# Two-block kernel: recurrent mixer's products reordered, block 2's set-up inside the second FFN, modulation products pinned

## Chip, cores and metric

One NeuronCore of a Trainium2 chip runs the whole kernel. The metric is the device time of one execution in microseconds; the median of three executions counts.

## What is computed

A token stream x of 256 tokens by 1024 features goes through two blocks, all in float32.

```python
# first block, two layers
x = x + mixer_a(rms_norm(x, norm_mix[0]))       # gated MLP with a 128x128 causal mix
x = x + conv_ffn(rms_norm(x, norm_ffn[0]))      # 1024 -> 2 x 3072 -> 1024
x = x + mixer_b(rms_norm(x, norm_mix[1]))       # recurrent mixer
x = x + conv_ffn(rms_norm(x, norm_ffn[1]))
h = rms_norm(x, norm_final)

# mixer_b, width 1536 in 6 heads of 256
g, xb = split(h @ w_in); g = gelu(g); xb = causal_conv(xb)      # 4 taps
r, i = sigmoid(xb @ w_a + b_a), sigmoid(xb @ w_x + b_x)         # by head
a = exp(8 * r * log_sigmoid(lam))
hs = scan(a, sqrt(1 - a**2) * i * xb)                           # along the tokens
return (hs * g) @ w_out

# second block
sh1, sc1, gt1, sh2, sc2, gt2 = split(silu(c) @ ada_w + ada_b)   # "modulation", v = 0 to 5
xn = rms_norm(h, mix_norm_g) * (1 + sc1) + sh1
h = h + gt1 * second_mixer(xn)              # sparse attention and an RWKV7 time mix
xn2 = rms_norm(h, moe_norm_g) * (1 + sc2) + sh2
return h + gt2 * moe(xn2)                   # router, 2 of 32 experts
```

## The kernel before

**Order of the work.** `first_block` (L695) runs `mixer_a`, `ffn` of layer 0, `mixer_b`, `setup2` and `ffn` of layer 1, then `final_norms`. `build` calls `router_setup` after it, then `second_mixer`, `finish_blocks` and `moe`. Each engine has a queue in order. Nobody writes that queue out by hand: a planner issues what it expects to be ready, and takes the earlier in program order where several are. So an instruction can run long before its place in the program, where its operands, its memory and its bank allow it. The change uses a call, `keep_in_program_order`, that places an instruction not before the one that its engine was given just before it in the program; later ones may still overtake both.

**Products.** Weights come by DMA on SyncE's queue in pieces of 512 KB (`wload`, L244). ScalarE copies each into a rounded high half and VectorE subtracts for the low half (`split_act`, L303 to L306); four split places of two pieces' halves make a ring. `mm3` (L267) makes one float32 product of three passes, L272 to L274. Feature products (`feats`, L286) have 256 token columns; output projections (`out_proj`, L391) have 512.

**Norms.** `ending` (L422) adds the residual by feature halves and calls `after(half)`, which for the mixers and FFNs transposes that half of x (`turned`, L371, L377) and splits it for the next stage. The row factors follow from sums of squares on ScalarE (L334) and Newton steps on VectorE (`newton`, L309). `factor_rows` (L347) puts them in a row: for each token half a diagonal on VectorE (L353) and a product with ones on TensorE (L354); both diagonals use one tile. `final_norms` (L1387) does this for two norms in a row and applies the modulation (L1407 to L1409).

**`mixer_b`** (L564) works in thirds P of four feature blocks: `conv_in` (two times 48 passes), `gelu_in` (the same), `gates` (48 passes), `recur` (ScalarE exponentials and roots, VectorE scans; L621 to L643) and the output projection (48 passes). `recur` of the last third goes by two halves. The order of the program is:

```python
for P in range(4):
    conv_in(P); mod_steps() if P == 0; gelu_in(P); y = recur(P - 1)
    gates(P); side(P); out_proj of y, with ending at P == 3
```

**Modulation.** `mod_load(v, h)` (L780) loads 512 columns of the modulation weights into four of eight tiles. With `summed` VectorE adds up the eight weighted rows at once (L795, L797), else TensorE does it in `mod_steps` (L810). `mod_steps` (L800) turns all halves loaded before it into columns: L822 for v = 0 and 1, L828 for v = 3 and 4, or into a row for v = 2 and 5 (L817, with a bias row loaded and the result written out on SyncE's queue, L816 and L819). It runs at the first step of each FFN, after `conv_in(0)` of `mixer_b`, and in `final_norms`. Loads stand at the end of steps: (0, 0), (0, 1), (2, 0), (2, 1) in FFN 0, (4, 0) and (4, 1) unsummed in `mixer_b`, (3, 0), (3, 1), (5, 0), (5, 1) in FFN 1.

**`setup2`** (L842) zeroes two images in DRAM from a zero tile (L847, L849), loads parameter rows on GpSimd's queue and transposes them (`turn`, L191 to L196), derives columns (L861 to L863), calls `setup_rwkv` (L872: masks, and four transposes for the head table at L909, each with a bank of its own and a copy at L910) and loads two gains. `router_setup` (L1510) loads the router's weights and makes a row and its broadcast with small products (L1523, L1526).

Of the kernel before, what the change touches and what calls it, by code (L numbers as in the profile page):

```python
# [7 lines left out]
F32 = mybir.dt.float32  # L8
# [3 lines left out]
ALU = mybir.AluOpType  # L12
# [5 lines left out]
NT = 2  # L18
# [88 lines left out]
class Net:  # L107
# [415 lines left out]
    def ffn(self, hT, ss, layer, side, after):  # L523
# [6 lines left out]
        with self.scope() as p:  # L530
            acc, hd, rows = None, {}, None
            for s in range(13):
                if s < 12:
# [30 lines left out]
    def mixer_b(self, hT, ss, side, after):  # L564
# [8 lines left out]
        with self.scope() as p:  # L573
# [72 lines left out]

            acc = todo = out_ss = None
            for P in range(4):
                if P < 3:
                    xb, xs = conv_in(P)  # L650
                if P == 0:
                    self.mod_steps()
                if P < 3:
                    gg = gelu_in(P)
                y = recur(P - 1, *todo, 4 if P < 3 else 2) if P > 0 else None
                if P < 3:
                    todo = (xb, gg, *gates(P, xs))
                side(P)
                if P > 0:
                    acc = acc or self.banks()  # L660
                    it = self.items(y, w_out, 4 * (P - 1), 4)
                    self.out_proj(acc, it[:2], P == 1)
                    done = None
                    if P == 3:
                        done, out_ss = self.ending(acc, after)
                    self.out_proj(acc, it[2:], False, done)
            return out_ss
# [27 lines left out]
    def first_block(self):  # L695
# [5 lines left out]
        with self.scope() as self.mod_scope:  # L701
# [39 lines left out]
            def then(i):  # L741
# [5 lines left out]
            ss = self.mixer_b(hT, ss, loads({0: (4, 0), 1: (4, 1)}), then(2))  # L747
            self.setup2()
            final, banks = Scope(self), []
            ss = self.ffn(hT, ss, 1, loads({1: (3, 0, 1), 3: (3, 1, 1), 5: (5, 0, 1), 8: (5, 1, 1)}),  # L750
                          lambda half: self.final_half(final, half, banks))
            self.final_norms(final, ss, banks)
# [27 lines left out]
    def mod_load(self, v, h, summed=False):  # L780
# [17 lines left out]
        self.mod_ready.append((v, h, rows, part))  # L798

    def mod_steps(self, psum=None):  # L800


        nc, psum = self.nc, psum or self.bank
        for v, h, rows, part in self.mod_ready:
            by = self.ones[:, :1]
            if part is None:
                ps, by = psum(), self.sel4
                for k in range(8):
                    q = 32 * (k % 4)
                    nc.tensor.matmul(ps[q:q + 32], self.c_b[:, k], rows[k], start=k < 4, stop=k >= 4, skip_group_check=True)  # L810
                part = self.mod_scope.tile([128, 512], name="mpart")
                nc.scalar.copy(part, ps)
            ps, c0 = psum(), v * D + 512 * h
            if v in (2, 5):
                row = self.mod_scope.tile([1, 512], name="mrow")
                nc.sync.dma_start(row, self.A["ada_b_2"][:, c0:c0 + 512])  # L816
                nc.tensor.matmul(ps[:1], by, part, start=True, stop=True)  # L817
                nc.vector.tensor_tensor(row, row, ps[:1], ALU.add)  # L818
                nc.sync.dma_start(self.mod[v // 3:v // 3 + 1, 512 * h:512 * h + 512], row)  # L819
            elif v < 2:  # L820
                for k in range(4):
                    nc.tensor.matmul(ps[:, k:k + 1], part[:, 128 * k:128 * k + 128], by, start=True, stop=True)  # L822
                to = self.mod_col[:, v, 4 * h:4 * h + 4]
                nc.vector.tensor_tensor(to, to, ps[:, :4], ALU.add)
            else:

                for k in range(8):
                    nc.tensor.matmul(ps[64 * h:64 * h + 64, k:k + 1], part[:, k::8], by, start=True, stop=True)  # L828
# [13 lines left out]
    def setup2(self):  # L842
        nc, A, c = self.nc, self.A, self.const
        self.x_img = [self.dram.tile([32, self.UNIT], F32, name=f"x_img{i}") for i in range(2)]
        with self.scope() as p:
# [9 lines left out]
            v(A[f"rwkv_{n}_2"]) for n in ("w0", "a0", "k_k", "k_a")] + [  # L855
            A["rwkv_r_k_2"][0].rearrange("(n h) p -> n (h p)", h=2), v(A["rwkv_ln_w_2"]), v(A["rwkv_ln_b_2"])], nc.gpsimd)
        self.rc = turn()

# [4 lines left out]
        nc.vector.tensor_scalar(rd[:, 23:27], rc[:, 27:31], -1.0, 1.0, op0=ALU.mult, op1=ALU.add)  # L863
        self.setup_rwkv()

        self.qkg = c.tile([128, 2], F32, name="qkg")
        for i, n in enumerate(("q_norm_g_2", "k_norm_g_2")):
            for h in range(2):
                nc.gpsimd.dma_start(self.qkg[HS[h], i:i + 1], A[n].rearrange("o d -> d o"))
        nc.vector.tensor_scalar(self.qkg[:, 0:1], self.qkg[:, 0:1], 0.125, None, op0=ALU.mult)  # L870

    def setup_rwkv(self):  # L872
# [31 lines left out]
        for b in range(4):  # L904
            nc.vector.tensor_copy(self.hsel[:, b, 2 * b:2 * b + 2], hi[:, :2])
        self.hexp = self.par2.tile([8, 4, 128], F32, name="hexp")
# [480 lines left out]
    def final_norms(self, p, ss, banks):  # L1387
# [13 lines left out]
        self.mod_steps()  # L1401
        gcol, shcol = self.mod_cols(0, 1, self.mix_g)
# [30 lines left out]
    def second_mixer(self):  # L1433
# [10 lines left out]
        with ExitStack() as es:  # L1444
# [14 lines left out]
            with self.scope(first) as zz, self.scope(second) as px:  # L1459
# [51 lines left out]
    def router_setup(self):  # L1511
# [10 lines left out]
        for k in range(8):  # L1522
            nc.tensor.matmul(ps[:1, :36], self.sh2[:, k:k + 1], rw[:, k], start=k == 0, stop=k == 7)  # L1523
        nc.vector.tensor_tensor(row[:1], row[:1], ps[:1, :36], ALU.add)
        ps = self.bank()
        nc.tensor.matmul(ps[:, :36], self.ones[:1], row[:1], start=True, stop=True)  # L1526
        self.r_add = c.tile([128, 36], F32, name="r_add")
# [259 lines left out]
```

## Time and profile before

| what | us |
|---|---|
| median of 3 executions | 1501.7 (1501.48 to 1502.59) |
| the profiled execution | 1502.12 |
| its span, first to last instruction | 1500.4 |
| recurrent mixer, about | 371 to 503 |
| second FFN, about | 508 to 727 |
| second mixer, about | 741 to 1030 |
| experts | to the end |

The profiled execution is 0.42 us over the median, and 1.7 us of it lie around the span. The page gives each engine's busy time and the chain that ended last; the views by stretch, the timelines and the waits are taken from the same execution. PE is TensorE's products, PEld its weight loads, DVE VectorE, ACT ScalarE, POOL GpSimd, SP SyncE. Overlapping starts are normal: products are pipelined and their ends are modelled.

### The profile page before, as it was taken

What the parts mean: (1) busy time and instruction counts of PE and PEld (TensorE: products, weight loads), DVE (VectorE), ACT (ScalarE), POOL (GpSimd) and SP (SyncE); (2) the same over time, 40 slices, a digit from 0 to 9 for tenths busy, and PEclk for the clock granted to TensorE, in tenths of its full rate; (3) what the DMA queues carried; (4) which work ended last, traced back from release to release, by engine and by line L of the source; (5) the groups of instructions that cost most, each with busy time, mean ns of one, the idle gap of its engine ahead of it and who ended that gap; (6) DMA issues with size and microseconds to landing.
All of it is one profiled execution on the core that took longest, in us unless ns stands there. A gap on an engine that the chain in (4) does not pass through costs nothing.

```text
span 1500.4 us, 22885 instructions
## 1 busy us (share of the span) xinstructions
PE 1371.2 (91%) x9085; PEld 1042.1 (69%) x9085; DVE 852.7 (57%) x1628; ACT 615.2 (41%) x955; POOL 32.2 (2%) x63
## 2 busy tenths in 40 slices
PE   7999999999999899999999899998978878879785
PEld 6778999999998689999798688887413313234131
DVE  5796798778788789878859742775201101101011
ACT  6644555556688555555575544552100000000000
POOL 3000000000001000000000100001000000000000
PEclk9999999999999999999899795999999989999998
DMA  9898586555555578563243352487999999999997
GB/s 318 282 327 277 158 274 215 187 187 160 170 182 184 172 272 275 187 191 109 72 153 113 99 121 86 170 336 308 390 421 420 420 420 421 421 421 419 421 419 253
DMA packets 165573, 391.18 MB, mean 261 GB/s; under 512 B 19440, under 2 KB 101100, under 8 KB 141780
## 3 DMA queue, kind: packets, MB, share of 16 engines
q1 hardware_dynamic: 153124, 383.64, 70.2%
q10 hardware_dynamic: 11136, 4.53, 1.3%
q0 software_dynamic: 1200, 1.49, 0.4%
q8 instruction: 73, 1.20, 0.3%
q14 instruction: 40, 0.33, 0.1%
HBM read 386.19 MB, written 3.43 MB: 260 GB/s over the span
## 4 chain that ended last, share of the span: by engine, by line
PE 58%; DMA 29%; DVE 7%; ACT 4%; issue 2%; SPq 0%; POOL 0%; DVEq 0%; ACTq 0%
DMA arena<-expert_w_gate 12%; PE ps L272 9%; PE ps L273 9%; PE ps L274 9%; DMA arena_w<-expert_w_gate 7%; DMA arena_w<-expert_w_down 6%; PE pc L273 5%; PE pc L272 5%; PE pc L274 5%; DMA arena<-expert_w_down 3%; PE pg L272 2%; PE pg L274 2%; PE pg L273 2%; DVE arena_r L306 2%; ACT arena_r L305 1%
## 5 line engine op out<-in xcount | busy, mean ns | idle before, releaser
L305 ACT ACTIVATE arena_r<-arena 128x1024 fp32r<-128x1024 f32 (+2 forms) x330 | 328.9, 1008 | 287.1 <-PE ps L273 73.1
L306 DVE TENSOR_TENSOR arena_r<-arena,arena_r 128x1024 fp32r<-128x1024 f32 (+2 forms) x330 | 376.9, 1154 | 119.2 <-ACT arena_r L305 115.8
L272 PE MATMUL ps<-arena_r,arena_r 128*128 128x256 f32 (+2 forms) x1192 | 353.7, 297 | 1.0 <-DVE arena L818 1.0
L273 PE MATMUL ps<-arena_r,arena_r 128*128 128x256 f32 (+2 forms) x1192 | 352.9, 296 | 1.1 <-DVE arena_r L306 1.1
L274 PE MATMUL ps<-arena_r,arena_r 128*128 128x256 f32 (+2 forms) x1192 | 352.4, 296 | 0.6 <-DVE arena_r L306 0.6
L272 PEld LDWEIGHTS ps<-arena_r,arena_r 128*128 128x128 f32 (+1 forms) x1192 | 229.3, 192 | 10.4 <-issue 3.5
L273 PEld LDWEIGHTS ps<-arena_r,arena_r 128*128 128x128 f32 (+1 forms) x1192 | 229.2, 192 | 7.2 <-DVE arena_r L306 1.5
L274 PEld LDWEIGHTS ps<-arena_r,arena_r 128*128 128x128 f32 (+1 forms) x1192 | 229.2, 192 | 5.6 <-DVE arena_r L306 0.8
L1709 PE MATMUL pc<-arena 128*32 128x512 f32 x576 | 144.4, 672 | 34.1 <-DMA arena<-expert_w_up 18.9
L272 PE MATMUL pc<-arena_r,arena_r 128*128 128x512 f32 x344 | 136.0, 399 | 5.3 <-ACT arena_r L305 3.4
L273 PE MATMUL pc<-arena_r,arena_r 128*128 128x512 f32 x344 | 135.9, 395 | 0.4 <-DVE arena_r L306 0.4
L274 PE MATMUL pc<-arena_r,arena_r 128*128 128x512 f32 x344 | 134.2, 393 | 0.0
L1709 PE MATMUL pc<-arena_w,arena 128*32 128x512 f32 x448 | 117.4, 663 | 15.8 <-DMA arena_w<-expert_w_gate 9.8
L1716 DVE TENSOR_TENSOR arena<-arena,pc 128x512 f32<-128x512 f32 x8 | 5.5, 688 | 204.6 <-PE pc L1709 204.6
L1692 ACT ACTIVATE arena<-ps,mod_col,moe_g 128x128 f32<-128x128 f32 x32 | 14.7, 458 | 246.1 <-DVE arena L1694 246.1
L1709 PEld LDWEIGHTS pc<-arena 128*32 128x32 f32 x576 | 31.4, 120 | 99.1 <-issue 37.1
L272 PE MATMUL pg<-arena_r,arena_r 128*128 128x256 f32 (+1 forms) x312 | 95.0, 306 | 2.0 <-DVE arena L916 1.8
L273 PE MATMUL pg<-arena_r,arena_r 128*128 128x256 f32 (+1 forms) x312 | 94.7, 305 | 1.1 <-DVE arena_r L306 1.1
L274 PE MATMUL pg<-arena_r,arena_r 128*128 128x256 f32 (+1 forms) x312 | 95.1, 306 | 0.2 <-DVE arena_r L306 0.2
L521 DVE SCALAR_TENSOR_TENSOR arena<-arena 128x255 f32<-128x255 f32 (+2 forms) x228 | 94.4, 477 | 0.2
L1735 PE MATMUL pc<-arena 128*32 128x512 f32 (+2 forms) x320 | 74.7, 584 | 11.5 <-DMA arena<-expert_w_down 7.6
L272 PEld LDWEIGHTS pc<-arena_r,arena_r 128*128 128x128 f32 x344 | 65.2, 190 | 19.8 <-ACT arena_r L305 5.1
(451 smaller groups left out, 1688.2 us busy)
## 6 DMA issues: line engine op xcount, KB each, us to landing
arena<-f_w_up SPq DMA_DIRECT2D x96, 512.0 KB, 3.9
arena<-expert_w_gate SPq DMA_DIRECT2D x41, 1024.0 KB, 19.9
arena<-expert_w_down SPq DMA_DIRECT2D x34, 1024.0 KB, 19.9
arena_w<-expert_w_up SPq DMA_DIRECT2D x33, 1024.0 KB, 19.9
arena<-expert_w_up SPq DMA_DIRECT2D x31, 1024.0 KB, 19.9
arena_w<-expert_w_down SPq DMA_DIRECT2D x26, 1024.0 KB, 19.9
arena<-ada_w SPq DMA_DIRECT2D x48, 512.0 KB, 5.6
arena<-f_w_down SPq DMA_DIRECT2D x48, 512.0 KB, 4.2
```

The costliest lines, as they stand in the source:

```text
L272: nc.tensor.matmul(acc, ah, bh, start=first, stop=False, **kw)
L273: nc.tensor.matmul(acc, ah, bl, start=False, stop=False, **kw)
L274: nc.tensor.matmul(acc, al, bh, start=False, stop=last, **kw)
L305: self.nc.scalar.activation(hi, src, AF.Copy)
L306: self.nc.vector.tensor_tensor(lo, src, hi.bitcast(F32), ALU.subtract)
L521: nc.vector.scalar_tensor_tensor(o[:, i:], src[:, :S - i], w[k - 1 - i], o[:, i:], op0=ALU.mult, op1=ALU.add)
L1692: nc.scalar.activation(xg[:, k], ps[:, j], AF.Identity, scale=g, bias=sh)
L1709: nc.tensor.matmul(gu[i][es], xg[:, kk, es], ws[e][:, k], start=kk == 0, stop=kk == 7, skip_group_check=True)
L1716: tt(hd, hd, gu[1], ALU.mult)
L1735: nc.tensor.matmul(o[es], hT[:, k0 + k, es], ws[e][:, k, f0 - c0:f0 - c0 + n], start=k0 + k == 0, stop=k0 + k == 3, skip_group_check=True)
```

## The change

`mixer_b` gets a written order in which the gates come next to the recurrence and the output projection a third later. `mod_steps` runs at the third step of each FFN, at the ninth of the second one, after the first gates of `mixer_b`, and in `second_mixer` after the value projection, in place of `final_norms`; all its products are pinned. `router_setup` goes there too, with pinned products. `setup2` runs in two parts at the fifth and eleventh step of the second FFN. `factor_rows` has two diagonal tiles. The head table is made in one bank with one copy. The Newton steps of `final_norms` work on both token halves in one tile of two columns.

```diff
@@ factor_rows
-            by = p.tile([128, 128], name="fdiag")
+            by = p.tile([128, 128], name="fdiag", bufs=2)
@@ ffn
-                if s == 0:
+                if s == 2 or (s == 8 and layer == 1):
                     self.mod_steps()
@@ mixer_b
-            for P in range(4):
...
+            acc = []
+
+            def out(P, y, done=None):
+                acc.extend(() if acc else self.banks())
+                it = self.items(y, w_out, 4 * P, 4)
+                self.out_proj(acc, it[:2], P == 0)
+                self.out_proj(acc, it[2:], False, done)
+
+            xb, xs = conv_in(0)
+            gg = gelu_in(0)
+            todo = (xb, gg, *gates(0, xs))
+            side(0)
+            self.mod_steps()
+            xb, xs = conv_in(1)
+            side(1)
+            gg = gelu_in(1)
+            y = recur(0, *todo, 4)
+            todo = (xb, gg, *gates(1, xs))
+
+            xb, xs = conv_in(2)
+            out(0, y)
+            y = recur(1, *todo, 4)
+            rg = gates(2, xs)
+            todo = (xb, gelu_in(2), *rg)
+            out(1, y)
+            done, out_ss = self.ending(acc, after)
+            out(2, recur(2, *todo, 2), done)
             return out_ss
@@ first_block
-            self.setup2()
...
+            def beside(s):
+                late(s)
+                if s == 4:
+                    turn.append(self.setup2())
+                if s == 10:
+                    self.setup2_columns(*turn)
+
+            ss = self.ffn(hT, ss, 1, beside, lambda half: self.final_half(final, half, banks))
@@ mod_steps, router_setup
+    def pinned(self, *args, **kw):
+
+        self.tc.keep_in_program_order(self.nc.tensor.matmul(*args, **kw))
...
-                    nc.tensor.matmul(ps[q:q + 32], self.c_b[:, k], rows[k], start=k < 4, stop=k >= 4, skip_group_check=True)
+                    self.pinned(ps[q:q + 32], self.c_b[:, k], rows[k], start=k < 4, stop=k >= 4, skip_group_check=True)
...
         self.mod_ready = []
+        if "mpart" in self.mod_scope.tags:
+            self.mod_scope.drop("mpart")
@@ setup2, which now returns turn; setup2_columns is what stood after turn()
-        self.rc = turn()
...
+    def setup2_columns(self, turn):
+        nc = self.nc
         self.rc = turn()
...
-        for b in range(4):
-            ps = self.psum()
-            nc.tensor.transpose(ps[:8, :128], self.hsel[:, b], self.ident)
-            nc.vector.tensor_copy(self.hexp[:, b], ps[:8, :128])
+        ps = self.psum()
+        for b in range(4):
+            nc.tensor.transpose(ps[:8, 128 * b:128 * b + 128], self.hsel[:, b], self.ident)
+        nc.vector.tensor_copy(self.hexp, ps[:8].rearrange("p (a b) -> p a b", b=128))
@@ final_norms
+        w2, y2, u2 = (self.stile(NT, f"rms2_{n}") for n in "wyu")
         for t in range(NT):
-
-            w, y, u = (self.stile(1, f"rms2_{n}") for n in "wyu")
+            w = w2[:, t:t + 1]
...
-            self.newton(y, w, u)
-            rs.append(y)
-        self.mod_steps()
+            rs.append(y2[:, t:t + 1])
+        self.newton(y2, w2, u2)
@@ second_mixer
                 self.rwkv_proj(v, 2, "pg")
+                self.mod_steps()
+                self.router_setup()
@@ build
-        net.router_setup()
```

## Rows read from the trace of the kernel before

**Rows 1.** The page, part 1: busy us, share of the span, instructions.

```profile
PE 1371.2 (91%) x9085; PEld 1042.1 (69%) x9085; DVE 852.7 (57%) x1628; ACT 615.2 (41%) x955; POOL 32.2 (2%) x63
```

**Rows 2.** By stretch: us; busy PE, PEld, DVE, ACT, POOL; granted clock, DMA share, GB/s.

```profile
387.00:474.00 87.00, 86.42 (x674) 84.08 (x674) 76.53 (x108) 70.22 (x102) 0.00 (x0) 1.00 0.53 168
474.00:508.00 34.00, 27.09 (x119) 19.70 (x119) 28.00 (x59) 26.82 (x45) 5.65 (x11) 0.99 0.63 205
...
546.00:727.00 181.00, 180.98 (x1253) 168.87 (x1252) 156.30 (x225) 101.77 (x134) 2.58 (x6) 1.00 0.59 191
...
811.00:846.00 35.00, 28.51 (x172) 24.28 (x172) 31.59 (x80) 22.63 (x38) 1.93 (x3) 0.89 0.38 121
...
1060.00:1460.00 400.00, 328.60 (x1650) 127.36 (x1644) 54.52 (x104) 18.74 (x42) 0.00 (x0) 0.94 1.01 420
```

**Rows 3.** Waits of TensorE, 474 to 508 us: total us, times, longest.

```profile
PE pc L272 <- ACT arena_r L305: 3.4, 2, 1.7
PE ps L909 <- DVE arena_r L367: 2.5, 1, 2.5
...
PE pc L273 <- DVE arena_r L306: 0.4, 1, 0.4
```

**Rows 4.** Timeline of VectorE, 472 to 481 us: start, us, instruction, [idle before].

```profile
472.67 0.93 DVE L847 MEMSET arena<- 128x1040 f32 x1 [0.17 <-DVE arena_r L306]
...
480.92 0.26 DVE L888 TENSOR_SCALAR arena<-m_d,m_fr 128x64 f32<-128x64 f32 x1 [1.97 <-DMA x_img<-arena]
```

**Rows 5.** Timeline of TensorE, 503 to 508 us.

```profile
503.74 0.25 PE L195 MATMUL ps<-ident,arena 43*128 43x43 f32 x1
...
507.73 0.55 PE L272 MATMUL ps<-arena_r,arena_r 128*128 128x256 f32 x1
```

**Rows 6.** Busy time in short stretches, columns as in rows 2.

```profile
505.00:510.00 5.00, 2.90 (x12) 2.47 (x13) 4.85 (x21) 1.78 (x4) 0.00 (x0) 0.70 0.33 105
510.00:515.00 5.00, 5.00 (x42) 5.00 (x42) 2.72 (x14) 1.18 (x2) 0.00 (x0) 0.96 0.32 105
...
528.00:531.00 3.00, 3.00 (x16) 1.13 (x9) 2.40 (x7) 0.67 (x2) 0.00 (x0) 0.51 1.04 383
...
534.00:537.00 3.00, 3.00 (x17) 3.00 (x17) 2.10 (x5) 1.58 (x2) 0.00 (x0) 0.56 0.02 5
```

**Rows 7.** Chain that ended last, modulation products: start, us, what.

```profile
385.00 0.95 PE pc L817 x2
...
525.04 2.01 PE pc L828 x16
...
531.43 2.01 PE pc L828 x16
...
727.73 3.49 PE pc L828 x32
```

**Rows 8.** Timeline of TensorE, 726 to 742 us.

```profile
737.34 1.12 PE L1523 MATMUL pc<-rw,mod_col 128*1 128x36 f32 x16
...
740.84 0.55 PE L272 MATMUL ps<-arena_r,arena_r 128*128 128x256 f32 x1 [1.01 <-DVE arena L818]
```

**Rows 9.** Timeline of VectorE, 727 to 738 us.

```profile
727.33 0.69 DVE L420 TENSOR_TENSOR arena<-arena,pc 128x512 f32<-128x512 f32 x1 [0.74 <-PE pc L274]
729.77 0.15 DVE L830 TENSOR_TENSOR mod_col<-mod_col,pc 64x8 f32<-64x8 f32 x1 [1.76 <-PE pc L828]
729.85 0.68 DVE L1382 TENSOR_TENSOR arena<-arena 128x512 f32<-128x512 f32 x1
...
733.13 0.20 DVE L1396 TENSOR_SCALAR rms_w<-ss,ss 128x1 f32<-128x1 f32 x1
...
737.45 0.29 DVE L353 TENSOR_SCALAR arena<-ident,rms_y 128x128 f32<-128x128 f32 x1 [0.30 <-PE pc L354]
```

**Rows 10.** Timeline of ScalarE, 730 us.

```profile
730.62 0.63 ACT L334 ACTIVATE arena<-arena 128x512 f32<-128x512 f32 x1 [1.69 <-DVE arena L1382]
```

**Rows 11.** Groups of instructions of VectorE: count, busy us, mean ns.

```profile
L797 DVE SCALAR_TENSOR_TENSOR arena<-arena 128x512 f32<-128x512 f32 x70 | 51.2, 745 | 0.1
```

More of the change, by code (lines that the diff above doesn't have):

```diff
@@ L645, in recur @@
                 return y
-            acc = todo = out_ss = None
-            for P in range(4):
-                if P < 3:
-                    xb, xs = conv_in(P)
-                if P == 0:
-                    self.mod_steps()
[L653 to L666, printed above, removed]
+            acc = []
[22 more added lines that the diff above has]
+            out(2, recur(2, *todo, 2), done)
             return out_ss
@@ L747, in first_block @@
             ss = self.mixer_b(hT, ss, loads({0: (4, 0), 1: (4, 1)}), then(2))
-            self.setup2()
-            final, banks = Scope(self), []
-            ss = self.ffn(hT, ss, 1, loads({1: (3, 0, 1), 3: (3, 1, 1), 5: (5, 0, 1), 8: (5, 1, 1)}),
-                          lambda half: self.final_half(final, half, banks))
+            final, banks, turn = Scope(self), [], []
+            late = loads({1: (3, 0, 1), 3: (3, 1, 1), 5: (5, 0, 1), 8: (5, 1, 1)})
+            def beside(s):
[5 more added lines that the diff above has]
+            ss = self.ffn(hT, ss, 1, beside, lambda half: self.final_half(final, half, banks))
             self.final_norms(final, ss, banks)
@@ L816, in mod_steps @@
                 nc.sync.dma_start(row, self.A["ada_b_2"][:, c0:c0 + 512])
-                nc.tensor.matmul(ps[:1], by, part, start=True, stop=True)
+                self.pinned(ps[:1], by, part, start=True, stop=True)
                 nc.vector.tensor_tensor(row, row, ps[:1], ALU.add)
@@ L821, in mod_steps @@
                 for k in range(4):
-                    nc.tensor.matmul(ps[:, k:k + 1], part[:, 128 * k:128 * k + 128], by, start=True, stop=True)
+                    self.pinned(ps[:, k:k + 1], part[:, 128 * k:128 * k + 128], by, start=True, stop=True)
                 to = self.mod_col[:, v, 4 * h:4 * h + 4]
@@ L827, in mod_steps @@
                 for k in range(8):
-                    nc.tensor.matmul(ps[64 * h:64 * h + 64, k:k + 1], part[:, k::8], by, start=True, stop=True)
+                    self.pinned(ps[64 * h:64 * h + 64, k:k + 1], part[:, k::8], by, start=True, stop=True)
                 to = self.mod_col[64 * h:64 * h + 64, v]
@@ L856, in setup2 @@
             A["rwkv_r_k_2"][0].rearrange("(n h) p -> n (h p)", h=2), v(A["rwkv_ln_w_2"]), v(A["rwkv_ln_b_2"])], nc.gpsimd)
+        self.setup_rwkv()
+        self.qkg = c.tile([128, 2], F32, name="qkg")
+        for i, n in enumerate(("q_norm_g_2", "k_norm_g_2")):
+            for h in range(2):
+                nc.gpsimd.dma_start(self.qkg[HS[h], i:i + 1], A[n].rearrange("o d -> d o"))
+        nc.vector.tensor_scalar(self.qkg[:, 0:1], self.qkg[:, 0:1], 0.125, None, op0=ALU.mult)
+        return turn
+    def setup2_columns(self, turn):
+        nc = self.nc
         self.rc = turn()
@@ L863, in setup2 @@
         nc.vector.tensor_scalar(rd[:, 23:27], rc[:, 27:31], -1.0, 1.0, op0=ALU.mult, op1=ALU.add)
[L864 to L870, printed above, removed]
+        self.hexp = self.par2.tile([8, 4, 128], F32, name="hexp")
+        ps = self.psum()
+        for b in range(4):
+            nc.tensor.transpose(ps[:8, 128 * b:128 * b + 128], self.hsel[:, b], self.ident)
+        nc.vector.tensor_copy(self.hexp, ps[:8].rearrange("p (a b) -> p a b", b=128))
     def setup_rwkv(self):
@@ L905, in setup_rwkv @@
             nc.vector.tensor_copy(self.hsel[:, b, 2 * b:2 * b + 2], hi[:, :2])
-        self.hexp = self.par2.tile([8, 4, 128], F32, name="hexp")
-        for b in range(4):
-            ps = self.psum()
-            nc.tensor.transpose(ps[:8, :128], self.hsel[:, b], self.ident)
-            nc.vector.tensor_copy(self.hexp[:, b], ps[:8, :128])
     def mix(self, dst, ps, m, n=128):
@@ L1398, in final_norms @@
             nc.vector.tensor_scalar(w, w, sg[t][1], 0.5 / D, op0=ALU.add, op1=ALU.mult)
-            self.newton(y, w, u)
-            rs.append(y)
-        self.mod_steps()
+            rs.append(y2[:, t:t + 1])
+        self.newton(y2, w2, u2)
         gcol, shcol = self.mod_cols(0, 1, self.mix_g)
@@ L1522, in router_setup @@
         for k in range(8):
-            nc.tensor.matmul(ps[:1, :36], self.sh2[:, k:k + 1], rw[:, k], start=k == 0, stop=k == 7)
+            self.pinned(ps[:1, :36], self.sh2[:, k:k + 1], rw[:, k], start=k == 0, stop=k == 7)
         nc.vector.tensor_tensor(row[:1], row[:1], ps[:1, :36], ALU.add)
         ps = self.bank()
-        nc.tensor.matmul(ps[:, :36], self.ones[:1], row[:1], start=True, stop=True)
+        self.pinned(ps[:, :36], self.ones[:1], row[:1], start=True, stop=True)
         self.r_add = c.tile([128, 36], F32, name="r_add")
```

## The prediction

> **What bounds the kernel now.** I read the page first, then the stretches. TensorE is busy 91% of the span, VectorE 57%, ScalarE 41% [rows 1]. The busy table by stretches [rows 2] shows different limits. In the recurrent mixer (387 to 474 us) and in the second FFN (546 to 727 us) TensorE has next to no idle time (0.6 and 0.0 us), with VectorE at 76.5 of 87 and 156.3 of 181 us. At 474 to 508 us, the mixer's end, TensorE works 27.1 of 34 us. From 811 to 846 us, inside the second mixer, VectorE works 31.6 of 35 us and TensorE has gaps. From 1060 us on the DMA engines are full (share 1.01): the experts' weights set the end. They can't start sooner than buffers come free, which the TensorE work before them decides, so I carry every microsecond won or lost before 1040 us to the end, one for one.
>
> So a product costs its full time in the two dense stretches, and an idle wait is worth its full time at their borders. The change moves products from the second border into the dense stretches and takes waits out of the first.
>
> **Mixer's end, the recurrence.** TensorE waits here for the last third's output: 3.4 us on ScalarE's high half and 0.4 on VectorE's low half [rows 3]. One reason stands in VectorE's queue: the set-up of block 2 already runs there, its zero tile at 472.67 us, and a mask instruction waits 1.97 us for the DMA that writes these zeros [rows 4], ahead of the recurrence's own instructions. The change takes the set-up away and puts the gelu products of the last third behind its gates. The recurrence then has these 96 products and the next 48 beside it, not the 48 alone; the other two thirds keep at least the cover that they have. I expect 1 us of the 3.8 to remain: -2.8, bounds -3.8 and 0, since VectorE was already 88% busy in this mixer.
>
> **Mixer's end, the set-up.** TensorE stands in its own queue behind one transpose for the columns and four for the head table, from 503.74 us [rows 5] to 507.73: 2.5 us of it is a wait for the norm's last half, which holds the banks [rows 3]. The FFN's first products could begin at 503.74. They need the first half of the normed tokens alone, and the second follows well before they (48 x 0.12 = 5.8 us) are over. -4.0 us. The five transposes come back in the FFN at some 0.12 each: -3.4, bounds -4.0 and -1.5. The clock was low just then (0.70 of full, against 0.96 in the 5 us after [rows 6]), which should go with the stall: -1.3, priced below, bounds -1.3 and 0.
>
> In the FFN the set-up's VectorE work (some 4 us with the wait) and eleven GpSimd-queue DMAs lie beside products. VectorE has 25 us free there [rows 2], and POOL does 2.6 us in 181. Cost 0. With that cover gone it would be the 1.97 us wait and 2 us of small instructions. The DMAs pass no other GpSimd work of weight; SP's row loads and writes move along with their products, and no product waits for them.
>
> **Modulation's products.** Each half vector (v, h) costs TensorE its own set [rows 7]: 16 one-column products with 64-column weights take 2.01 us from the unsummed route and 3.49/2 = 1.75 from the summed one, the one-row pair 0.95. Moved between stages: (0,0) from the mixer to the first FFN, (4,0) from the second FFN to the mixer, which changes no sum; and out of the border at 727 us into the dense FFN, (3,0) and (3,1) at 1.75 each and (5,0) at 0.95. That is +4.4 us, fully exposed, as TensorE has no idle time there.
>
> **Clock.** [...] In 534 to 537 us 17 instructions ran where the full rate (42 in 5 us, one per 0.12) gives 25: 8 x 0.12 = 1.0 us. That row holds only part of the low stretch, so I take 1.3 a fall. [...] I expect 2.7 falls against 2: +0.9, bounds -2.6 (no fall) and +2.6 (four).
> [...]
>
> **Border of the second FFN.** The last residual starts at 727.33, right behind the last FFN product; block 2's first product at 740.84 us [rows 8, 9], 13.5 us later. VectorE's queue [rows 9] shows why: the final norm's multiply behind that residual runs only at 729.85, because a modulation add waits 1.76 us for its products; the first statistic is taken at 733.13; and the second diagonal, at 737.45, waits for the first one's product, which shares its tile. With the products gone, the multiply ends at 728.7, and ScalarE's squares (0.63 us each [rows 10], 0.8 with the read-out, an estimate) for one quarter and two halves end near 731.0. What is left of the statistics takes 0.4, eleven Newton steps on two columns 1.65 (0.15 each; 0.20 by the statistic's row, overlapping), both diagonals 0.3: 733.4. From the second diagonal's end to the first product pass 3.1 us now, and stay, with 0.2 for the second diagonal's product: 736.7. That is -4.1, bounds -5.5 and -1.0, as weight splits share VectorE. TensorE then idles longer, but its clock was at 0.5 here before too; I charge nothing for that.
>
> **Router and (5,1) in the second mixer.** They are now behind the value projection, near 811 us: 0.95 and 1.12 [rows 7, 8] plus a small pair, 2.6 us with their hand-over. The pair waits for an add in VectorE's full queue, and the group norm's products of the time mix stand behind, as their bank frees with these adds. TensorE already waits 6.5 us in that stretch for VectorE and ScalarE, so part is hidden: +1.7, bounds 0 and +2.6.
>
> **Loads.** The unsummed (4,0) held four of the eight tiles of modulation weights until its products ran. They now run in the mixer, so the load and the weighted sum of (3,0), 8 x 0.745 = 6.0 us of VectorE [rows 11], can come into the mixer, where VectorE has about 10 us in 87 free. +0.6, bounds 0 and +6.0.
>
> The second tile for the diagonals elsewhere, the single evacuation of the head table and the dropped tile move nothing that TensorE waits for: 0.
>
> **Sum.** -2.8 - 3.4 - 1.3 + 4.4 + 0.9 - 4.1 + 1.7 + 0.6 = -4.0 us. The profiled execution took 1502.1 us (span 1500.4), 0.4 above the median of 1501.7 that is to be compared; so 1497.7 us. 0.2%, 3.0 us here, is about what a measurement of this kernel can tell from no change.
>
> **Rivals.**
> 1. No clock falls from the moved products (0.17): -3.5 against my sum, 1494.2. For it: the one-row pair among the mixer's products ran in a stretch granted full clock, and all of 387 to 474 us was too [rows 2]. [...]
> 2. The border doesn't shorten (0.16): the norm's small instructions and the splits share one queue, and products no longer fill the wait. That term is then -1.0 and the time 1500.8, no change to be told.
> 3. VectorE becomes the mixer's bound (0.13), which is slower than before. The 6.0 us of weighted sums come into a queue with 10 us free in 87; once more than that is wanted before an output projection, TensorE waits in order. The recurrence's 2.8 are not won, the 6.0 are exposed (5.4 over my 0.6), and a clock fall follows the gap, 1.3: -4.0 + 9.5 = +5.5, 1507.2. Against: at 88% VectorE cost TensorE no more than 0.6 us in 87 [rows 2].
> 4. The order hardly changes, since the planner already placed these products where they became ready (0.04): 1501.7.
> 5. The router's products are wholly hidden and the mixer's wait vanishes (0.05): 1495.
>
> **How the numbers follow.** My forecast has 0.45, its own range 1494.5 to 1501; about 0.32 of it lies under 1498.7. Faster: 0.32 + 0.17 + 0.05 = 0.54. Same: 0.13 + 0.14 (rival 2) + 0.04 = 0.31. Slower: 0.13 + 0.02 = 0.15. The range 1491.5 to 1504 takes in all cases but rival 3 and the far end of rival 1.
>
> **What would show it.** Right: no transposes of the set-up before the second FFN; its first product within a microsecond of the norm; under 1.5 us of waits in the third output projection; a border of 9 to 10.5 us; the FFN longer by about 5 us. Wrong: TensorE waits on VectorE's splits in the mixer before 474 us, a border over 12 us, or a second mixer longer by over 3 us.

## The result and the profile of the changed kernel

The changed kernel takes 1511.99 us in the median (1511.61 to 1513.57), the kernel before 1501.59 beside it: a ratio of 1.0071, 95% interval 1.0056 to 1.0086. It is 10.4 us slower; 1497.7 was forecast, and the time lies outside the range given with it (1491.5 to 1504).

The page has the same number of matrix products and 9.6 us less busy time on TensorE than [rows 1]:

```profile
PE 1361.6 (90%) x9085; PEld 1039.0 (69%) x9085; DVE 854.2 (56%) x1620; ACT 616.9 (41%) x956; POOL 32.1 (2%) x63
```

So nothing was added. TensorE stands still longer, and the table by stages says where. A stage begins with its first product (the second border with the second FFN's last), read from the timeline of TensorE of one profiled execution each; the last two columns are runs 1 and 11 of the section below.

| stage, us | before | changed | ps banks | adds pinned |
|---|---|---|---|---|
| up to the first FFN | 162.5 | 163.4 | 162.3 | 164.4 |
| first FFN and its norm | 208.4 | **219.3** | 211.6 | 209.1 |
| recurrent mixer and its norm | 136.8 | 134.6 | 133.8 | 133.3 |
| second FFN, to its last product | 219.2 | 208.2 | 218.2 | 210.4 |
| border to block 2 | 14.0 | **26.1** | 11.1 | 12.0 |
| second mixer, up to the routing | 285.4 | 286.5 | 285.4 | 283.8 |
| routing, experts, end of the span | 474.1 | 473.8 | 476.7 | 474.1 |
| span | 1500.4 | 1511.9 | 1499.2 | 1487.0 |

The changed kernel loses 10.9 us ahead of the mixer and 12.1 at the second border. It wins 11.0 in the second FFN, out of which block 2's modulation products and the two falls of the clock (0.51 and 0.56 of full [rows 6]) have gone, and 2.2 in the mixer. The first loss stands in the timeline of TensorE, 366 to 383 us:

```profile
366.67 0.95 PE L816 MATMUL pc<-ones,arena 128*128 128x1 f32 x8
...
368.59 0.95 PE L816 MATMUL pc<-ones,arena 128*128 128x1 f32 x8
...
370.00 0.95 PE L816 MATMUL pc<-ones,arena 128*128 128x1 f32 x8
...
371.82 0.40 PE L274 MATMUL pc<-arena_r,arena_r 128*128 128x512 f32 x1
381.98 1.11 PE L377 MATMUL ps<-ident,arena 128*128 128x128 f32 x4 [9.77 <-DVE arena L420]
382.75 0.56 PE L272 MATMUL ps<-arena_r,arena_r 128*128 128x256 f32 x1
```

L816 is the pinned product. The products of (1,0), (1,1) and (0,0) stand behind the FFN's third step in the program, near 200 us; here they run at its very end, and then TensorE waits 9.77 us for a residual, L420. Why the residual is late shows in VectorE's timeline of the same stretch:

```profile
364.95 0.68 DVE L420 TENSOR_TENSOR arena<-arena,pc 128x512 f32<-128x512 f32 x1
...
367.73 0.48 DVE L809 TENSOR_SCALAR arena<-arena 128x512 f32<-128x512 f32 x1
...
371.73 0.48 DVE L809 TENSOR_SCALAR arena<-arena 128x512 f32<-128x512 f32 x1
372.12 6.71 DVE L811 SCALAR_TENSOR_TENSOR arena<-arena 128x512 f32<-128x512 f32 x10
...
381.25 0.68 DVE L420 TENSOR_TENSOR arena<-arena,pc 128x512 f32<-128x512 f32 x1
```

The two weighted sums of (2,0) and (2,1) (L809 and L811, 2 x 0.48 + 14 x 0.745 = 11.4 us [rows 11]) run here, in a queue that the norm needs; in the kernel before they began at 177 and 214 us, inside the FFN (VectorE's timeline of the kernel before):

```profile
176.89 0.48 DVE L795 TENSOR_SCALAR arena<-arena 128x512 f32<-128x512 f32 x1
...
213.95 0.48 DVE L795 TENSOR_SCALAR arena<-arena 128x512 f32<-128x512 f32 x1
```

A sum needs one of four tiles, and those were held by the halves whose products had not run.

The second border, TensorE's timeline, 723 to 752 us:

```profile
723.10 1.92 PE L816 MATMUL pc<-arena 128*32 128x512 f32 x16
...
725.53 0.39 PE L274 MATMUL pc<-arena_r,arena_r 128*128 128x512 f32 x1
...
738.57 2.05 PE L816 MATMUL pc<-ones,arena 128*64 128x1 f32 x16 [5.51 <-DVE arena L811]
...
748.49 1.20 PE L354 MATMUL pc<-arena,ones 128*128 128x128 f32 x4 [6.07 <-DVE arena L353]
751.61 1.01 PE L272 MATMUL ps<-arena_r,arena_r 128*128 128x256 f32 x3 [1.92 <-ACT arena_r L1432]
```

The same thing one step further back: the unsummed (4,1) held four of the eight weight tiles until its products ran at 723.10 us. Only then could the last two halves be loaded (SyncE's queue, eight loads from 724.20 us) and summed (VectorE's timeline: first operations of the sums of (3,1) and (5,1), and the diagonals that end the norm's factors):

```profile
724.20 14.62 SPq L801 DMA_DIRECT2D arena<-ada_w  x8
```

```profile
730.82 0.47 DVE L809 TENSOR_SCALAR arena<-arena 128x512 f32<-128x512 f32 x1
...
737.28 0.48 DVE L809 TENSOR_SCALAR arena<-arena 128x512 f32<-128x512 f32 x1
...
748.07 0.47 DVE L353 TENSOR_SCALAR arena<-ident,rms_y 128x128 f32<-128x128 f32 x2
```

What went as foretold: the mixer's end, and a second FFN without an idle wait. TensorE's waits from 474 to 518 us, to be read against [rows 3], and the second FFN in the busy table (columns as in [rows 2]):

```profile
PE pc L272 <- ACT arena_r L305: 0.9, 1, 0.9
PE ps L274 <- DVE arena_r L306: 0.9, 1, 0.9
PE ps L377 <- DVE arena L420: 0.3, 1, 0.3
```

```profile
517.00:727.00 210.00, 209.98 (x1487) 195.31 (x1487) 165.16 (x252) 122.33 (x164) 0.00 (x0) 1.00 0.53 164
```

The second 0.9 belongs to the last third's input; the output projection keeps 0.9 of 3.8 us, and no set-up stands before the second FFN, which runs at full clock throughout.

### The profile page after: what moved, and what is told of

Read it like the earlier page. It is cut to its first block, busy times and chain, and to the rows that moved or that the text cites. A ratio compares the mean times of both kernels' runs of the same rounds, so it can differ in the third digit from the quotient of the medians.

```text
span 1511.9 us, 22880 instructions
## 1 busy us (share of the span) xinstructions
PE 1361.6 (90%) x9085; PEld 1039.0 (69%) x9085; DVE 854.2 (56%) x1620; ACT 616.9 (41%) x956; POOL 32.1 (2%) x63
## 4 chain that ended last, share of the span: by engine, by line
PE 58%; DMA 29%; DVE 9%; ACT 2%; issue 2%; SPq 0%; DVEq 0%; ACTq 0%
DMA arena<-expert_w_gate 12%; PE ps L273 9%; PE ps L272 9%; PE ps L274 9%; DMA arena_w<-expert_w_gate 7%; DMA arena_w<-expert_w_down 6%; PE pc L272 5%; PE pc L273 5%; PE pc L274 5%; DMA arena<-expert_w_down 3%; PE pg L273 2%; PE pg L272 2%; PE pg L274 2%; DVE arena_r L306 2%; DVE arena L811 1%
## 5 line engine op out<-in xcount | busy, mean ns | idle before, releaser
L272 PE MATMUL ps<-arena_r,arena_r 128*128 128x256 f32 (+2 forms) x1192 | 351.1, 296 | 1.9 <-ACT arena_r L1432 1.9
L274 PE MATMUL ps<-arena_r,arena_r 128*128 128x256 f32 (+1 forms) x1192 | 351.1, 295 | 1.4 <-DVE arena_r L306 1.3
L273 PE MATMUL ps<-arena_r,arena_r 128*128 128x256 f32 (+2 forms) x1192 | 351.3, 295 | 1.0 <-DVE arena_r L306 1.0
L272 PEld LDWEIGHTS ps<-arena_r,arena_r 128*128 128x128 f32 (+1 forms) x1192 | 227.7, 191 | 8.9 <-ACT arena_r L1432 2.2
L273 PEld LDWEIGHTS ps<-arena_r,arena_r 128*128 128x128 f32 (+1 forms) x1192 | 228.0, 191 | 7.2 <-DVE arena_r L306 1.4
L274 PEld LDWEIGHTS ps<-arena_r,arena_r 128*128 128x128 f32 x1192 | 227.8, 191 | 6.9 <-DVE arena_r L306 2.0
L1735 PE MATMUL pc<-arena 128*32 128x512 f32 x576 | 140.5, 659 | 34.7 <-DMA arena<-expert_w_up 18.4
L1735 PE MATMUL pc<-arena_w,arena 128*32 128x512 f32 x448 | 114.6, 637 | 20.2 <-DMA arena_w<-expert_w_gate 10.2
L1766 DVE TENSOR_TENSOR arena<-pc,arena 128x512 f32<-128x512 f32 (+2 forms) x17 | 11.2, 661 | 118.9 <-PE pc L1761 118.9
```

Source lines behind the costliest of these rows:

```text
L272: nc.tensor.matmul(acc, ah, bh, start=first, stop=False, **kw)
L273: nc.tensor.matmul(acc, ah, bl, start=False, stop=False, **kw)
L274: nc.tensor.matmul(acc, al, bh, start=False, stop=last, **kw)
L1735: nc.tensor.matmul(gu[i][es], xg[:, kk, es], ws[e][:, k], start=kk == 0, stop=kk == 7, skip_group_check=True)
L1766: tt(ys[:, sl], yo[f0 // 512][:, f0 % 512:f0 % 512 + n], gt2[:, sl], ALU.mult)
```

## The experiments

**Theory.** The kernel divides PSUM into four banks named pc and four named ps. From its second step an FFN's output accumulators hold all four pc banks, until their last residuals. Modulation's products take a pc bank too. Behind the first step they get one; behind the third or ninth they can't run before the FFN ends. Their operands' tiles stay full meanwhile, and loads and sums pile up at the border. Rivals: the pins make the planner put the products last; or the second border grew through the norm's own new order.

**1. Other banks.**

```diff
-                    self.mod_steps()
+                    self.mod_steps(self.psum)
```

> Edit: the changed kernel, but modulation's products in the two FFNs take their PSUM bank from the four banks of the FFN's inputs (ps), not from the four of its output (pc). Bank theory: from the second step on the FFN's four output accumulators hold all of pc until its last residuals, so the products put behind that step could only run at the FFN's end (366 and 723 us), and the weighted sums that wait for their tiles ran in VectorE's queue at the border. With ps banks the products run inside the FFNs, the 9.8 us wait at 372 us goes (below 1 us), the second border falls from 26 us to 11 to 14, and the time is 1488 to 1493. Pin theory (the pins make the planner put the products last): nothing moves, 1512. Border theory (the second border is long because of the norm's own new order): only the first border is won back, about 1501.

Measured: 1500.38 us, ratio 0.9988 (0.9979 to 0.9998). The products ran at 203.5, 548.4 and 657.6 us. The first border's wait is gone and the second border is 11.1 us (waits of TensorE at each):

```profile
PE ps L377 <- DVE arena L420: 0.3, 1, 0.3
...
PE pc L354 <- DVE arena L353: 5.8, 1, 5.8
PE ps L272 <- ACT arena_r L1432: 1.5, 1, 1.5
PE ps L377 <- DVE arena L1406: 1.1, 1, 1.1
```

Both places behave as the bank theory has it; the time does not: 7 to 12 us more than I expected. By the median that is the border theory's figure, but the stages contradict that theory, since the second border shrank by 15. Two things took most of the gain. The clock fell four times inside dense stretches, behind each set of moved products: to 0.66 of full from 205 to 210 and from 410 to 415 us, 0.69 from 555 to 560 and 0.66 from 660 to 665. The first and the last, columns as in [rows 2]:

```profile
205.00:210.00 5.00, 5.00 (x22) 4.18 (x22) 3.88 (x9) 0.62 (x2) 0.00 (x0) 0.66 0.44 136
...
660.00:665.00 5.00, 5.00 (x15) 3.58 (x14) 3.96 (x7) 0.00 (x0) 0.00 (x0) 0.66 0.38 113
```

At the price found below, 1.5 us each, that is some 6 us, and the products cost their own time as well: with two of the falls the second FFN takes 218.2 us, 10 more than in the changed kernel, where they ran after it. Another 2.9 us came behind the routing (476.7 against 473.8), in code that the edit does not touch.

**2. No pins.**

```diff
-        self.tc.keep_in_program_order(self.nc.tensor.matmul(*args, **kw))
+        self.nc.tensor.matmul(*args, **kw)
```

> Edit: the changed kernel with plain products in place of the pinned ones. Bank theory: the products still wait for a pc bank, same places, 1511 to 1513. Pin theory: they run where they stand in the program, both borders shrink, 1490 to 1500.

Measured: 1513.2 us, ratio 1.0076 (1.0059 to 1.0093), with the same wait at the same place:

```profile
PE ps L377 <- DVE arena L420: 9.8, 1, 9.8
```

The pins have no part in it.

**3. Products behind the first step.**

```diff
-                if s == 2 or (s == 8 and layer == 1):
+                if s == 0:
```

> Edit: the changed kernel with modulation's products behind the first step of both FFNs (before the output takes the pc banks), as the kernel before had them, still pinned, and without the call behind the ninth step, so that the products of (3,0), (3,1), (5,0) and (5,1) all run in the second mixer. Bank theory: products run near 175 and 530 us, the weighted sums inside the FFNs, both borders short: 1488 to 1496, with 4 to 6 us more in the second mixer than in the changed kernel. Pin theory: 1512. Border theory: about 1501.

Here (3,0), (3,1), (5,0) and (5,1) are multiplied in the second mixer from tiles of a scope that ends with the first block, so that the second mixer may take their space for its own tiles (this is read from the code, not from a trace; the changed kernel reads (5,1) alone that way). The values came out different, the experts' part grew, and the whole took 4447 us, which says nothing here. The stages ahead of it can be read: first-border wait 0.3 us, second border 11.1, second FFN 210.4 (granted clock 1.00 in every five microseconds from 505 to 620 us); block 2 began at 725.98 us, against 740.84 in the kernel before. It agrees with the bank theory for the borders only.

**4. One term of eight.**

```diff
-            for k in range(8):
+            for k in range(1 if (v, h) in ((2, 0), (2, 1), (3, 1), (5, 1)) else 8):
```

> Edit: the changed kernel, whose weighted sums of the half vectors (2,0), (2,1), (3,1) and (5,1) leave out seven of their eight terms; modulation's products stay where they are, at the ends of the FFNs. This tells whether it is the sums in VectorE's queue or the late products themselves that cost the borders. Sums: the 9.8 us wait at 372 us falls to 1 or 2 us, the second border to 14 to 18 us, in all 1490 to 1496. Products (or their loads): under 3 us won, 1509 to 1512.

Measured: 1495.46 us, ratio 0.9966 (0.9956 to 0.9976), some 16 us under the changed kernel with the products still at the FFNs' ends (365.99 and 711.09 us). This kernel leaves out work and computes other values; it serves only to price the sums. TensorE's waits at the first border, 360 to 390 us, are down to

```profile
PE ps L377 <- DVE arena L420: 0.3, 1, 0.3
```

So at the first border the price is the sums in VectorE's queue, not the late products. At the second, 8.4 us go with the sums (26.1 to 17.7); 6.6 more stay above the 11.1 of run 1, where products and loads run inside the FFN as well, and no run parts these two.

**5. The cause alone, in the kernel before.**

```diff
-                if s == 0:
+                if s == 2 - 2 * layer:
```

> Edit: the kernel before, with one number changed: modulation's products behind the third step of the first FFN instead of the first (no pins, nothing else of the change). Bank theory: they find no bank until the FFN's end, the weighted sums of (2,0) and (2,1) move to the first border, TensorE waits some 10 us there: 1509 to 1514. If something else of the change made the first border long: 1500 to 1503.

Measured: 1513.0 us, ratio 1.0067 (1.005 to 1.0084). Waits of TensorE, 360 to 390 us:

```profile
PE ps L377 <- DVE arena L420: 8.7, 1, 8.7
```

As the bank theory expected: one number, the place of one call, costs 10 us; the first FFN and its norm take 218.7 us instead of 208.4.

**6 and 7. The two parts that were meant to gain, alone.** The mixer's order in the kernel before, with modulation's call behind the first gates, so that (4,0) comes into the mixer:

```diff
-            for P in range(4):
...
+            xb, xs = conv_in(2)
+            out(0, y)
+            y = recur(1, *todo, 4)
+            rg = gates(2, xs)
+            todo = (xb, gelu_in(2), *rg)
```

> Edit: the kernel before, with nothing but the recurrent mixer's new order (and the call for modulation's products behind its first third). Cover theory (the prediction's): TensorE's 3.8 us of waits in the third output projection come from too few products beside the last recurrence; they fall to 1.5 us or less, the set-up's transposes still stand before the second FFN, and the time is 1498 to 1500.5. Queue theory: those waits come from the set-up's instructions in VectorE's queue; they stay at 3 to 4 us, 1501 to 1503. VectorE theory: the weighted sums of (3,0) come into the mixer and stall its projections, 1504 to 1508.

Measured: 1499.52 against 1502.37 us, ratio 0.998 (0.9971 to 0.999): -2.9 us. The set-up in two steps in the kernel before, with the one bank for the head table and the dropped tile of the change:

```diff
-            self.setup2()
...
+                if s == 4:
+                    turn.append(self.setup2())
+                if s == 10:
+                    self.setup2_columns(*turn)
```

> Edit: the kernel before, with nothing but block 2's set-up in two steps of the second FFN (and the dropped tile, without which it has no room). Prediction's terms: 3.4 us from the transposes before the second FFN and 1.3 us of clock there, 1496 to 1498.5. Queue theory: the recurrence's 3.8 us of waits go too, as VectorE no longer runs the set-up ahead of it, 1493 to 1496. Rival: the norm's second half or the first products' clock takes the place of the transposes, 1499.5 to 1502.

Measured: 1497.98 us, ratio 0.9973 (0.9961 to 0.9986): -4.4 us. The waits of TensorE, 476 to 510 us, of the mixer's order first and then of the set-up, separate cover and queue:

```profile
PE ps L916 <- DVE arena L917: 2.0, 1, 2.0
...
PE pc L272 <- ACT arena_r L305: 0.6, 1, 0.6
...
PE pc L274 <- DVE arena L910: 0.3, 1, 0.3
```

```profile
PE pc L272 <- ACT arena_r L305: 2.9, 2, 1.7
PE ps L377 <- DVE arena L420: 1.9, 1, 1.9
PE pc L273 <- DVE arena_r L306: 0.4, 1, 0.4
```

With the order alone the projection's 3.8 us fall to 0.9 though the set-up still sits in VectorE's queue; without the set-up they stay at 3.3. Cover was the reason, and the set-up's work on VectorE at most 0.5 us of it.

**8 and 9. A version with the products where TensorE waits anyway.** Products behind the first step of both FFNs, where there are banks; (3,0), (3,1), (5,0) and (5,1) unpinned in the second border, which in run 1 had a 5.8 us wait:

```diff
-                if s == 2 or (s == 8 and layer == 1):
+                if s == 0:
...
+        late = self.mod_border()
...
         rows = self.factor_rows(rs, p)
+        late()
...
-                self.mod_steps()
                 self.router_setup()
```

Here mod_border issues the products and late their adds.

> Edit: the changed kernel, with modulation's products behind the first step of both FFNs (there they get a bank at once), and those of (3,0), (3,1), (5,0) and (5,1) laid into the second border, unpinned, before the final norm's factors, with their adds behind the factor rows; the router's set-up stays in the second mixer. Bank theory: the sums run inside the FFNs; the border's products fill a wait of 6 us that the run with ps banks showed there (TensorE on VectorE's Newton steps), so the border stays at 10.9 to 12 us and nothing is paid for them: 1488 to 1493. Rival: their adds and their clock lengthen the norm's chain, border 12.5 to 15 us, 1493 to 1498.

Measured: 1495.73 us, ratio 0.9949 (0.9931 to 0.9968), with a border of 16.2 us: the rival's case in the time, and a border still longer than the 12.5 to 15 that it gave. Then the router's set-up further back:

```diff
-                self.router_setup()
...
             qT, kT, vn = self.qkv(qkv, third)
+            self.router_setup()
```

> Edit: the run with the filled border, and the router's set-up, unpinned, behind the attention's inputs in the second mixer, where TensorE waits 2.9, 1.8 and 1.8 us in a row in the run with ps banks (835 to 843 us). If the router's products behind the value projection were exposed there (the second mixer up to the time mix's pairs took 100.8 us with them and (5,1), 97.6 in the kernel before), 1 to 3.3 us are won against the run with the filled border, 1486 to 1491. If that stretch is bound by VectorE and ScalarE anyway: within 1 us of that run.

Measured: 1493.5 us, ratio 0.9939 (0.9923 to 0.9956), 2.2 us under run 8, which the intervals do not separate, and above the 1486 to 1491 expected.

**10 and 11. What holds the border.** First the border's products pinned behind the last transposes:

```diff
-                    nc.tensor.matmul(cols[64 * h:64 * h + 64, k:k + 1], part[:, k::8], by, start=True, stop=True)
+                    self.pinned(cols[64 * h:64 * h + 64, k:k + 1], part[:, k::8], by, start=True, stop=True)
```

> Edit: the run with the late router, with the border's products of modulation pinned, so that they stand behind the last transposes of the final norm instead of ahead of them. In the run with the late router the border took 16.0 us (last FFN product to first product of block 2) and the last four transposes began 5.8 us after the others, behind those products; in the run with ps banks the border took 10.9 to 11.1. If the products' place ahead of the transposes is what lengthened it, the border falls to 11 to 12.5 us and the time to 1488.5 to 1491. Rival: at the border's lower clock the 4.4 us of products and their adds outlast the 6 us wait whatever their place, border 14 us or more, 1492 to 1495.

Measured: 1493.96 us, border 15.8: no gain, my expectation missed. VectorE's own waits, 718 to 732 us, said why. The planner had put the adds, which the program has behind the norm's factors, ahead of the norm's statistics, and VectorE stood there for the products:

```profile
DVE mod_col L874 <- PE pc L816: 3.3, 1, 3.3
...
DVE arena L874 <- PE pc L816: 0.5, 1, 0.5
```

So the adds were pinned too, on VectorE:

```diff
-                nc.vector.tensor_tensor(to, to, ps, ALU.add)
+                self.tc.keep_in_program_order(nc.vector.tensor_tensor(to, to, ps, ALU.add))
```

> Edit: the run with the pinned border products, with their four adds pinned on VectorE too, behind the two diagonals of the final norm. In the run before, VectorE reached the first of these adds at 721.1 us and stood 3.26 us for TensorE's products, and 0.54 us again, with the final norm's statistics queued behind; the diagonals came at 730.5, 11.0 us after the last multiply (719.4), against 6.8 us in the run with ps banks (727.1 to 733.9). If this queue is what lengthened the border, it falls from 15.8 to 11 to 12 us and the time to 1489 to 1491. If the products or the border's clock set it, whatever the adds' place: 15 us or more, 1493 to 1495.

Measured: **1487.81 us**, ratio 0.9902 (0.9887 to 0.9917), the fastest version here: 14.1 us under the kernel before, 24 under the changed one. The border is 12.0 us with four half vectors' products in it, and TensorE's waits in it, 717 to 730 us, are down to

```profile
PE ps L272 <- ACT arena_r L1459: 1.5, 1, 1.5
PE ps L377 <- DVE arena L1432: 1.1, 1, 1.1
```

**12 and 13. Do smaller sets spare the clock?** Run 1 with one half vector a step:

```diff
-                if s == 2 or (s == 8 and layer == 1):
-                    self.mod_steps(self.psum)
+                if 2 <= s <= 9:
+                    self.mod_steps(self.psum, 1)
```

> Edit: the run with ps banks, with the products of one half vector a step (steps three to ten) instead of all that are ready at once. That run showed four stretches of lower clock, each right behind a set of modulation's products (24, 44, 66 and 18 of them), and the kernel before none behind its set of 16 at 175 us. If it is the length of a set that brings the fall, at most two of the four stay, and 2 to 4 us are won against the run with ps banks: 1496 to 1499. If any such set does, more sets bring as many falls: 1500 to 1502.

Measured: 1502.08 us, ratio 0.9992 (0.9981 to 1.0003). The first case of the expectation failed, and the second gave the time (1500 to 1502) but not the rule, as not every set brought a fall: the four sets of eight products in the first FFN and the one-row pairs brought no fall (1.00 of full in every five microseconds from 165 to 370 us, and from 625 to 635 and from 675 to 685), but each set of sixteen or more in the second FFN did (0.69, 0.73 and 0.78 of full in the five microseconds behind 550, 570 and 590 us), and the mixer's set at 404 to 411 us once more (0.69 from 410 to 415). (The third set that the expectation counts as 66 was one of 48; 18 of them ran later, as the fourth.) With the router moved back as in run 9:

> Edit: the spread run, and the router's set-up behind the attention's inputs, unpinned, as in the run with the late router. 1.5 to 2.5 us under the spread run, as the late router was against the filled border; within 1 us of it if the stretch hides the router either way.

Measured: 1497.4 us, ratio 0.9962 (0.9947 to 0.9976), 4.7 us under run 12, more than expected. But its times spread from 1494.3 to 1501.6, and its profiled execution gained only 0.9 us of span, so I make nothing of the size.

## Why the prediction was wrong, point by point

**The step that failed** is in "Modulation's products": that moving (0,0) into the first FFN and (4,0) into the mixer "changes no sum", and that the others cost their own time in the dense stretch, +4.4 us. I took a product's place in the program for its place in time, and asked what a moved product would cost but not what it holds while it waits, nor which bank it would wait for. Both were there to read: the call stands one step behind the line that takes all pc banks. In its place the first FFN and its norm grew by 10.9 us, 10.2 of which run 5 gives with nothing else changed, and the second border by 12.1 instead of shrinking by 4.1.

**Loads.** Rival 3 had the mechanism, weighted sums in VectorE's queue, and the wrong place. Sums did come into the mixer, two rather than the one I counted ((3,0) and (5,0), begun at 422 and 451 us), and cost nothing visible: TensorE's waits from 474 to 518 us came to 2.1 us in all. Spread through that dense stretch, the two sums were free; at the first border, where TensorE waits for VectorE's next small result, two of them cost 9.8 us of their 11.4.

**Recurrence, -2.8.** The mechanism was right: the projection's waits fell from 3.8 to 0.9 us by cover, as argued. That run 6 was also 2.9 us faster as a whole is partly luck. In its profile the mixer and its norm are 1.2 us longer, since (4,0)'s products came in; the second FFN is 6.3 shorter, as they left it and the two falls of the clock with them (1.00 of full in every five microseconds from 515 to 620 us); the second border is 2.8 longer; and what lies behind it differs by -1.7 and +1.1. My side remark that one reason stood in VectorE's queue explains 0.5 us at most (run 7).

**Set-up, -3.4 and -1.3.** Right: -4.4 us for the two together (run 7), 4.0 of them in the mixer and its norm. No set-up transpose was left before the second FFN, and inside it they stand in a stretch without an idle wait.

**Border, -4.1.** -2.8 once the sums and products were out of it (14.0 to 11.1, run 1). The mechanism was right, the size too large; VectorE's 6.8 us from the last multiply to the diagonals stayed the limit. The term had too little behind the squares: 2.1 us from their end to the first diagonal (731.0 to 733.1), where run 1 took 4.1 (729.8 to 733.9). VectorE's timeline has two things there that the sum left out: a weight split of 1.08 us, and the Newton steps of the first of the two norms (L339 and L340, then one column at a time), which only x needs and which stand last in `final_norms`; the planner laid them between. Run 11 against run 10 shows how tight that queue is: four adds moved behind the norm's factors gave 3.8 us of border. The time fell by 6, but run 10's profile also has two falls of the clock, near 410 and 523 us (0.66 of full from 410 to 415 and from 522 to 527), that run 11's lacks (1.00 in both).

**Router and (5,1) in the second mixer, +1.7.** 0.0 in run 1 (285.4 us in both), +1.1 in the changed kernel: hidden nearly or wholly, within its bounds.

**Clock, +0.9.** The two falls of the kernel before, to 0.51 and 0.56 of full [rows 6], stand behind sets of sixteen one-column products (525.04 and 531.43 us [rows 7]), and I expected nearly one for each group of sets that the change moves. No run shows the 2.7 falls of that sum. In the changed kernel the products left the FFNs and no fall stood inside them (1.00 of full from 160 to 366 and from 517 to 727 us); the falls went to the longer borders, 0.50 of full from 380 to 385 and from 730 to 750 us, where TensorE was busy 3.02 of 5 and 6.85 of 20 us. Where the products did run in dense work, in run 1, there were four falls. The falls of runs 1 and 12 did not follow an idle gap: TensorE was busy 5.00 of 5.00 us in them and on both sides.

**The sum.** The terms for the mixer's end, -7.5 us, were worth -7.3 in the medians of runs 6 and 7, the first of them partly by luck. Run 1 has the products where I put them. Its profiled execution is 3.8 us ahead of the kernel before at the routing (the stages above), about the -4.0 that I summed, with a second border and clock worse than forecast and a router and sums better, so that the agreement is luck too. Of this 1.2 us are left at the end of the span and 1.3 in the medians; what takes the rest behind the routing I have not settled.

## What to carry to other kernels

Before an operation is moved, list what it must acquire (a bank, a tile) and what it keeps others from acquiring until it has run; then find who holds that at its new place. Cheap operations that free buffers belong ahead of the long holder of the scarce one, or in another pool. And when filler is laid into a wait, lay down its consumers too: in run 10 VectorE's queue carried a late product's wait, 3.3 us, to everything behind the add that reads it.

## What the hardware showed unasked

In these runs the clock did not answer to the program alone. Runs 8, 9, 10 and 11 have the same instructions in the second FFN, and the sixteen one-column products end near 523 us in each. In two of them the clock fell right there (0.66 of full in runs 9 and 10) and in two it did not (1.00 in runs 8 and 11); the busy table, 522 to 527 us, of run 9 and then of run 11 (columns as in [rows 2]):

```profile
522.00:527.00 5.00, 5.00 (x30) 4.99 (x30) 3.49 (x10) 0.95 (x3) 0.00 (x0) 0.66 1.01 360
```

```profile
522.00:527.00 5.00, 5.00 (x43) 4.99 (x43) 3.23 (x10) 2.43 (x4) 0.00 (x0) 1.00 1.01 368
```

The stage then takes 211.9 us in both with a fall and 210.4 in both without: 1.5 us a fall, by two profiled executions of each kind, where 1.3 was estimated. What decides between the two was not found; nor was it tried to give these products another form.

The end of the span also varies: from the last product to the end the profiled executions took 8.3 us (changed), 8.9 (before) and 11.7 (run 1), with the same code there. A profile's span can thus be 3 us off the stages that a change touches.
